# A reordered first stage, joined attention runs and fourteen instead of twelve gate pairs in a hybrid mixer layer

## The chip, the cores and the metric

The kernel runs on one core of one Trainium2 chip. The metric is the device time of one execution in microseconds (us). All data are float32; TensorE multiplies in float32r, and every operand is split into a high and a low part, so that one product of the mathematics is three matmuls (high x high, high x low, low x high).

## The reference

One layer of a diffusion backbone on 640 tokens: 512 sample tokens and 128 prompt tokens. In short:

```
mod = silu(c) @ w_ada + b_ada                    # sh1 sc1 g1 sh2 sc2 g2
h   = rmsnorm(x) * (1 + sc1) + sh1               # 640 x 1024
proj = h @ w_in                                  # ax ab ac | q ff fb i g | cq ck cv | du dv
y_a = ab * dwconv3(ac * ax)                      # gated convolution
y_b = hgrn2(q, ff, fb, i, g)                     # recurrence in both directions
y_c = attention(cq, ck, cv)                      # neighbourhood attention and context
y_d = du * (mixing of dv over 128 tokens)        # gated MLP
merged = sum over a, b, c, d of sigmoid(h @ w_gate + b_gate) * (y @ w_br)
x = x + g1 * (merged @ w_o)
h = rmsnorm(x) * (1 + sc2) + sh2
x = x + g2 * ((silu(g) * a) @ w_down),  (a, g) = dwconv3(h @ w_up)
```

Returned are the normalised x of both groups, the keys and values of the prompt, and the final states of the recurrence.

## The kernel before

**Layout.** h is kept transposed, features on the partitions, as `xh` (high part, 8 blocks of 128 features x 640 tokens) and `xl` (low part). A tile of a projection is 128 output features x 640 tokens, worked in two halves of 320 tokens (HC): 8 feature blocks x 3 matmuls x 2 halves = 48 matmuls of 320 columns. Weights come by DMA into one of three raw buffers (tag "raw"); `feat` (line 318) loads one and splits it: a ScalarE copy makes the high part, a VectorE subtraction (L329) the low part, in one of three weight buffers (tag "w"). `ahead` (line 1801) issues loads up to four units and preparations up to two units before use.

**The first stage.** x is loaded and normalised, transposed on TensorE, the first 16 column blocks of the modulation are computed from w_ada, and h is made. Meanwhile the first three tiles of w_in run on those feature blocks that are ready. The order of all this on every engine is a table written out by hand, BOOT (line 28), read token by token (line 1992) and kept as written. Its tokens: sq/sc (statistics and scaling of an x tile), tu/xo (transpose and copy out), ad, ev, tr, rd, md (one block of the modulation: product, copy, transpose, reduce, finish), adj, evj, ... (two blocks at once), hh/hm/hl (high part of h, h itself, low part), wh/wl (weight split), mikXY (one feature block k of tile i, high or low parts), warm (small matmuls that compute nothing). The order of the loads is LORD (line 22): numbers are blocks of w_ada (512 KB each), wih is half h of weight i (256 KB each). Behind them on SP's queue stand the small loads p2, lmask and four of st_in (lines 217 to 226), then the last four blocks of w_ada (L1981, regions A and B, used by adj3 and adj7).

**The middle.** The remaining sections of w_in follow in the order SECTIONS; jobs that are not plain products (HGRN, gMLP, convolution, attention, later columns of the modulation in `ada_cols`) are Python generators, which a clock of assumed TensorE time (`tick`, line 97) resumes between the products. The number that a job yields is the assumed time until it is resumed. The framework's scheduler then orders the instructions of each engine, except where the program asks to keep its order. Attention (line 701) works on 16 units (head x query block) in pairs; a round computes scores for the next pair (`s1`: TensorE L813 and L816, GpSimd L805, VectorE L820 and L822, ScalarE L823), normalises and transposes two units (`s2`: L829 to L835), and multiplies with the values (`s3`: L850, L856, L857).

**The gates.** There are 32 gate tiles, 8 for each branch in the order d, a, b, c. A plain gate tile (`gate_tile`, line 943) takes 48 matmuls for h @ w_gate and 12 for the branch. The 24 tiles of a, b and c run as 12 pairs (`g_pair`, line 1129): tiles n and n+4 share a scheme of seven instead of eight block products, on four quarters of h (two feature halves x two token halves) and sums of them. Each of the seven is 12 matmuls (L1098), and the branches take 24 (L1111). The operands x5, x6, x7 and x3 are sums of quarters, made in `g_operands` (line 992) from a copy of h in DRAM (`hdr`, line 931, stored at the end of the first stage, L2008), and split into high and low parts (`g_split`, L1023 and L1024). `g_operands` begins when the last d tiles have begun and the attention has ended. `gp_load` (line 1029) loads a pair's weights, `g_a`, `g_sums`, `g_b` and `g_c` prepare them, and from pair 0 on all engines keep the written order.

**After the gates** come w_o, the second normalisation, the up projection (in the same seven-product scheme, L1439) and the down projection (L1754). There, `low_dma` (line 1333) makes some low parts in another way: ScalarE writes minus the high part, and a DMA from GpSimd's queue adds the raw weight to it.

## Time and profile before

| | |
|---|---|
| median of 3 runs | 1042.53 us (1041.19 to 1042.62) |
| the profiled execution: time | 1042.9 us |
| its span, first to last instruction | 1041.1 us |
| mean granted TensorE clock | 0.996 |
| busy: TensorE, VectorE, ScalarE, GpSimd | 1021.4, 788.3, 528.9, 95.2 us |
| first stage ends (first L364 product) | 52.87 us |
| plain d tiles, last eight before the pairs | 280 to 357.7 us |
| attention ends (last L857) | 301.7 us |
| pairs | 357.7 to about 548 us |

The span holds the instructions; the execution's own time has some 1.8 us around them. The profile page gives busy times over the whole span; a view of waits says what an engine waited for; the chain follows back from the last instruction what released what; timelines list instructions in order of time, equal neighbours merged, with the start, the time that they take together, and in brackets the idle time before them. A name such as "L364 PE MATMUL g<-XH,w" is line 364, a matmul into PSUM tile g from XH and w. Line 146 is a helper that keeps the program's order: all first-stage instructions and all from the pairs on carry it, unless they have a line of their own.

### The profile page before, as it was taken

How to read it: one execution, taken by the hardware profiler on the slowest of the kernel's cores; microseconds unless marked ns; L12 is line 12 of the kernel's file. 1: busy time of each engine (PE TensorE's matmuls, PEld its weight loads, DVE VectorE, ACT ScalarE, POOL GpSimd, SP SyncE). 2: the span in 40 equal slices, each digit the busy share in tenths (PEclk: the TensorE clock that was granted, in tenths of full speed). 3: DMA queues.
4: the chain of work that ended last, by engine and by line, in shares of the span. 5: the costliest groups of instructions: out<-in, count | busy, mean ns of one | idle time of the engine just before them, and what ended most of it. 6: DMA issues, size and time to landing. Idle time of an engine off the chain costs nothing.

```text
span 1041.1 us, 18790 instructions
## 1 busy us (share of the span) xinstructions
PE 1021.4 (98%) x7638; PEld 962.9 (92%) x7638; DVE 788.3 (76%) x1280; ACT 528.9 (51%) x912; POOL 95.2 (9%) x139
## 2 busy tenths in 40 slices
PE   8899999999999999999999999999999999999997
PEld 6799989999889999999998899999999999888886
DVE  5559889789957467677768688998888887795834
ACT  6662343333243445445445377877677776632532
POOL 1000010201100000000000021211111111000201
PEclk9999999999999999999999999999999999999999
DMA  9954333453234122321258385666665558974212
GB/s 349 325 188 141 125 104 123 129 180 129 74 127 152 52 101 76 128 102 62 81 212 327 149 258 136 175 165 162 161 162 151 148 152 250 370 266 149 82 41 102
DMA packets 54296, 165.68 MB, mean 159 GB/s; under 512 B 7969, under 2 KB 14913, under 8 KB 52161
## 3 DMA queue, kind: packets, MB, share of 16 engines
q1 hardware_dynamic: 44432, 137.19, 37.8%
q0 software_dynamic: 9776, 27.28, 11.2%
q8 instruction: 60, 0.98, 0.4%
q14 instruction: 28, 0.22, 0.1%
HBM read 131.52 MB, written 21.52 MB: 147 GB/s over the span
## 4 chain that ended last, share of the span: by engine, by line
PE 91%; DVE 3%; DMA 3%; issue 1%; ACT 0%; SPq 0%; POOL 0%; POOLq 0%; DVEq 0%; ACTq 0%
PE g L364 19%; PE g L1439 19%; PE m L1098 14%; PE g L1754 8%; PE m L1754 6%; PE m L1439 5%; PE g L1111 4%; PE m L1234 3%; PE g L910 2%; PE g L1234 2%; PE m L525 1%; DMA S<-in_w_ada_dram 1%; PE m L850 1%; DMA B<-in_w_ada_dram 1%; DMA C<-in_w_ada_dram 1%; PE g L146 1%
## 5 line engine op out<-in xcount | busy, mean ns | idle before, releaser
L364 PE MATMUL g<-XH,w 128*128 128x320 f32 x832 | 201.2, 318 | 0.2 <-DVE MG L425 0.2
L364 PEld LDWEIGHTS g<-XH,w 128*128 128x128 f32 x832 | 142.9, 189 | 4.5 <-issue 3.7
L364 PE MATMUL g<-XL,w 128*128 128x320 f32 x416 | 129.7, 312 | 0.0
L364 PEld LDWEIGHTS g<-XL,w 128*128 128x128 f32 x416 | 78.9, 190 | 0.8 <-issue 0.5
L316 DVE TENSOR_TENSOR w<-raw,w 128x1024 fp32r<-128x1024 f32 x34 | 41.5, 1220 | 16.2 <-ACT w L315 15.5
L1754 PE MATMUL g<-w,XH 128*128 128x512 f32 (+1 forms) x216 | 47.5, 373 | 0.0
L315 ACT ACTIVATE w<-raw 128x1024 fp32r<-128x1024 f32 x34 | 35.8, 1052 | 20.5 <-PE g L1234 9.9
L1754 PEld LDWEIGHTS g<-w,XH 128*128 128x128 f32 x216 | 38.5, 188 | 7.6 <-ACT XH L1717 0.3
L1098 PE MATMUL m<-XH,w 128*128 128x320 f32 x192 | 45.0, 309 | 0.0
L146 DVE SCALAR_TENSOR_TENSOR X<-MG,p2t,X 128x641 f32<-128x641 f32 x44 | 38.9, 884 | 5.7 <-ACT X L146 4.8
L328 ACT ACTIVATE w<-raw 128x1024 fp32r<-128x1024 f32 (+1 forms) x26 | 29.4, 1130 | 22.2 <-PE g L364 7.5
L146 DVE SCALAR_TENSOR_TENSOR X<-X,p2t,X 128x641 f32<-128x641 f32 x44 | 38.9, 883 | 2.3 <-ACT X L146 1.0
L1754 PE MATMUL m<-w,XH 128*128 128x512 f32 (+1 forms) x180 | 40.2, 369 | 0.0
L1754 PE MATMUL g<-w,XL 128*128 128x512 f32 (+1 forms) x180 | 40.0, 373 | 0.0
L1439 PE MATMUL g<-XL,C 128*128 128x320 f32 x240 | 38.7, 310 | 0.4 <-ACT MG L146 0.4
L1439 PE MATMUL g<-XL,w 128*128 128x320 f32 x240 | 38.7, 310 | 0.2 <-DVE X L146 0.2
L1754 PEld LDWEIGHTS g<-w,XL 128*128 128x128 f32 x180 | 32.2, 188 | 6.8 <-DVE dt L1765 0.6
L329 DVE TENSOR_TENSOR w<-raw,w 128x1024 fp32r<-128x1024 f32 (+1 forms) x26 | 33.8, 1301 | 5.8 <-ACT w L328 5.6
L1439 PEld LDWEIGHTS g<-XL,C 128*128 128x128 f32 x240 | 35.9, 188 | 1.1 <-ACT MG L146 1.1
L1439 PEld LDWEIGHTS g<-XL,w 128*128 128x128 f32 x240 | 35.9, 188 | 0.8 <-issue 0.4
L1754 PEld LDWEIGHTS m<-w,XH 128*128 128x128 f32 x180 | 31.3, 189 | 5.3
L1754 PE MATMUL m<-w,XL 128*128 128x512 f32 (+1 forms) x150 | 33.2, 369 | 0.0
(544 smaller groups left out, 2704.9 us busy)
## 6 DMA issues: line engine op xcount, KB each, us to landing
raw<-in_w_up_dram SPq DMA_DIRECT2D x31, 512.0 KB, 5.1
raw<-in_w_gp_dram SPq DMA_DIRECT2D x18, 640.0 KB, 3.8
raw<-in_w_down_dram SPq DMA_DIRECT2D x22, 512.0 KB, 4.6
raw<-in_w_in_dram SPq DMA_DIRECT2D x19, 512.0 KB, 3.7
H<-in_w_adt_dram SPq DMA_DIRECT2D x16, 512.0 KB, 4.2
actd<-X POOLq DMA_DIRECT2D x22, 320.5 KB, 5.3
G<-in_w_up_dram SPq DMA_DIRECT2D x11, 512.0 KB, 4.8
X<-in_w_adt_dram SPq DMA_DIRECT2D x10, 512.0 KB, 4.1
```

The costliest lines, as they stand in the source:

```text
L146: r = f(*args, **kw)
L315: act(w[0], raw, AF.Copy)
L316: vec.tensor_tensor(w[1], raw, w[0].bitcast(F32), ALU.subtract)
L328: high = lambda: act(w[:, 0], raw, AF.Copy)
L329: low = lambda: vec.tensor_tensor(w[:, 1], raw, w[:, 0].bitcast(F32), ALU.subtract)
L364: mm(o, w[:, h, k0 + k, :], r(k)[:, s], start=(k == 0 and i == 0), stop=(k == kt - 1 and i == 2))
L910: mm(o, x(kx)[:, ts], w[:, h, k, :], start=(kx == 0 and i == 0), stop=(kx == 7 and i == 2))
L1098: mm(o, w[:, k, :], x[:, k, :], start=(first and k == 0 and j == 0), stop=(k == 3 and j == 2), skip_group_check=True)
L1111: mm(pb[:, c, 0:HC], w[:, h + k, :], y[:, x, k, s], start=(k == 0 and j == 0), stop=(k == 1 and j == 2))
L1234: mm(m, mh[k // 2][:, hx, k % 2, t * P:(t + 1) * P], wo[q][:, hw, k % 2, :], start=(k == 0 and i == 0), stop=(k == 7 and i == 2))
L1439: mm(o, w[:, k, :], x[:, k, :], start=(first and k == 0 and j == 0), stop=(k == 3 and j == 2), skip_group_check=True)
L1754: mm(acc[nh][t + c0 // 256][:, 0:c1 - c0], sl[k][hx][:, t * P:(t + 1) * P], w[:, hw, k, c0:c1], start=(kk_ == 0 and k == 0 and i == 0), st ...
```

## The change

- **First stage.** A new BOOT table of the same tokens. The first scalings of x come ahead of lbs and bada; 24 + 8 instead of 8 + 18 warm-up matmuls; the products are in another order (27 instead of 26 of the 72 pairs of products, and trj2, ahead of adj6). The loads of p2, lmask and st_in move from behind LORD to behind the stores of h at the end of the stage. h is stored by feature halves and token halves, four stores for two.
- **Fourteen pairs.** The d tiles 2, 3, 6 and 7 become two pairs in front of the others; the d tiles 0, 1, 4 and 5 stay plain. A d pair writes its product into the sum directly.
- **Operands of the pairs.** `g_operands` starts when the section cv is done. It loads three quarters of h into regions D and G as soon as attention has read cv, makes three sums after y_a (kept in written order), splits x7 once all scores are computed and x5, x6 after attention, then loads the fourth quarter over x5's source. Its sum for x3 is made in pair 0. y_b is kept in DRAM and brought back after the d pairs, y_c is stored by the attention.
- **Attention.** `s3` of a pair of units now stands directly ahead of `s1` of the next but one; a round yields 0.6 less.
- **Low parts.** The weights of ac, ax, ab and of the plain d tiles get their low part by `low_dma`.
- **Modulation columns 40 to 47**: gap 3 instead of 5, and 4 instead of 10 before the last step.

```diff
-sq0 sq1 lbs bada sc0a scv sc0b tu0a tu0b sq2 xo0a sc1b sc1a tu1b sq3 xo0b tu1a warm8 sc2a xo1a. sc2b tu2a xo1b
-sq4 tu2b sc3b ad0 sc3a xo2b. xo2a tu3b ev0. tu3a sc4b xo3b. ad8 sc4a xo3a. tr0 ev8 tu4a rd0 wh0a tr8 md0
...
+sq0 sq1 sc0a sc0b tu0a scv tu0b xo0a. sc1a sq2 bada tu1a warm24 xo0b xo1a sq3 sc1b lbs tu1b sc2a sq4
+sc2b tu2a xo1b tu2b ad0 xo2a. sc3a sc3b xo2b. tu3a sc4a ad8 ev0 wh0a sc4b tu4a xo3a tr0 ev8. xo4a. tr8
+rd0 tu4b rd8 md0 wh2a tu3b warm8 md8 xo4b hh0 ad1 wl2a xo3b. ev1 m20HH hm0 m00HH wh1a tr1 ad9 rd1 wl0a
+m20LH ev9. m10HH wl1a ad2 tr9 ev2. md1 m00LH rd9 m10LH hl0 ad10 md9 tr2 m00HL ev10 hh1 m10HL rd2 tr10
+md2 ad3 rd10 md10 m20HL hh2 hm1 m01LH m21LH m21HH hl1 m11LH ev3. m12HH wh0b m12LH hm2 m21HL wh1b m01HL
+wl0b m11HL wh2b m02HH m22HH wl1b m22LH m11HH hl2 ad11 tr3 ev11. wl2b m02LH m02HL m22HL rd3 tr11 md3 adj2
+rd11 md11 hh3 m12HL evj2 m01HH trj2 adj6 exp hm3 rdj2 hl3 m23HH m03HH m13LH evj6 m13HL m03HL mdj2 trj6
+lb m03LH adj3 rdj6 sig mdj6 m23HL evj3 m13HH trj3 m23LH hh4 rdj3 adj7 mdj3 hh5 m24LH evj7 m04LH trj7
...
+NPL = 2
+LOWD = ("ac", "ax", "ab", "d")
...
-    for r in (xreg0, xreg1):
-        vec.memset(r[:, 0:2 * XW].rearrange("p (i c) -> p i c", i=2)[:, :, D], (D * EPS) ** 0.5)
-    vec.memset(xe[4][:, D:XW], (D * EPS) ** 0.5)
+    for x in xe:
+        vec.memset(x[:, D:XW], (D * EPS) ** 0.5)
...
-    def feat(src, kt=8):
+    def feat(src, kt=8, dma=False):
...
-            low()
+            if dma:
+                low_dma(w[:, 1].rearrange("p a b -> p (a b)"), raw.rearrange("p a b -> p (a b)"))
+            else:
+                low()
...
-        R["yb"] = split_y("E", sg)
+        nc.sync.dma_start(ybd, split_y("D", sg).bitcast(F32))
         R["hgrn_done"] = True
-        R["yd"] = split_y("D", R["yt"])
+        R["yd"] = split_y("E", R["yt"])
...
         for u in range(0, 16, 2):
+            if u > 0:
+                s3(u - 2)
             if u < 14:
                 s1(u + 2)
-                yield HD[6]
+            else:
+                R["scores"] = True
+            yield HD[6]
             for i in range(2):
                 s2(u + i)
                 yield 1.2
-            s3(u)
-            yield HD[8]
+            yield HD[8] - 0.6
+        s3(14)
+        nc.sync.dma_start(ycd, yc.bitcast(F32))
...
-    PAIRS = [(bi, n) for bi in range(1, 4) for n in range(4)]
+    PAIRS = [(0, n) for n in range(NPL, 4)] + [(bi, n) for bi in range(1, 4) for n in range(4)]
...
     def g_operands():
-        while "yc" not in R:
+        while "cg" not in R:
             yield 1
...
+        d, g = region("D", [P, 2, 4, HC]), region("G", [P, 4, HC])
+        for x, h, c in ((d[:, 0], 0, 1), (d[:, 1], 1, 1), (g, 0, 0)):
+            nc.sync.dma_start(x, hdr[h, c])
+        while "ya" not in R:
+            yield 1
+        a21, a22, a11 = d[:, 0], d[:, 1], g
+        for o, x, y in ((a22, a21, a22), (a21, a11, a21), (a11, a22, a11)):
+            tc.keep_in_program_order(vec.tensor_tensor(o, x, y, ALU.subtract))
+            yield 2
...
+        for i, x, t, key in ((7, a21, "F", "scores"), (5, a22, "X1", "yc"), (6, a11, "X0", "yc")):
+            while key not in R:
+                yield 1
+            y = region(t, [P, 2, 4, HC], F32R)
+            gx["x"][i] = y[:, 0], y[:, 1]
             g_split(i, x)
             yield 1.5
+        nc.sync.dma_start(a22, hdr[1, 0])
+        gx["t3"] = a22, a11
...
-        r.append(region("G", [P, 10, P]) if p_ % 2 == 0 else rp.tile([P, 10, P], F32, tag="raw", name=nm("raw")))
+        r.append(region("G", [P, 10, P]) if p_ % 2 else rp.tile([P, 10, P], F32, tag="raw", name=nm("raw")))
...
-        return region("CBD"[i], [P, 5, 4, P], F32R)
+        return region("BCD"[i], [P, 5, 4, P], F32R)
...
-        ovec.tensor_tensor(c2(gt), pb, c2(gt), ALU.mult)
         mg = merged[n // 4][:, n % 4, :]
+        ovec.tensor_tensor(c2(gt if bi else mg), pb, c2(gt), ALU.mult)
+        if not bi:
+            return
         ovec.tensor_tensor(mg, mg, gt, ALU.add)
...
-            if PAIRS[q] == (1, 3):
-                R["yc"] = region("A", [P, 2, 2, T], F32R)
-                pool.dma_start(R["yc"], ycd)
+            if PAIRS[q] in ((0, 3), (1, 3)):
+                n_, t, y = ("yb", "E", ybd) if PAIRS[q][0] == 0 else ("yc", "A", ycd)
+                R[n_] = region(t, [P, 2, 2, T], F32R)
+                pool.dma_start(R[n_], y)
...
+        if q < 0:
+            t3, x6 = gx["t3"]
+            ovec.tensor_tensor(t3, t3, x6, ALU.add)
...
     for h in range(2):
-        nc.sync.dma_start(hdr[h], xT[h])
+        for c in range(2):
+            nc.sync.dma_start(hdr[h, c], xT[h][:, :, c * HC:(c + 1) * HC])
+    p2 = const.tile([P, 176], F32, name="p2t")
+    nc.sync.dma_start(p2, a["p2"])
...
```

More of the change, by code (lines that the diff above doesn't have):

```diff
@@ L216, in tile_step @@
             nc.sync.dma_start(adat[f // 2][:, f % 2], a["w_ada"][f])
-    p2 = const.tile([P, 176], F32, name="p2t")
-    nc.sync.dma_start(p2, a["p2"])
-    lmask = const.tile([P, 5, 32], U8, name="lmask")
-    lmr = region("G", [P, 5, 32])
-    nc.sync.dma_start(lmr, a["lmask"])
-    st_in = const.tile([P, 2, 2, 64], F32, name="st_in")
-    for par in range(2):
-        for d in range(2):
-            nc.sync.dma_start(st_in[64 * par:64 * par + 64, d],
-                              a["state_hgrn"][0, 0, d, par::2].rearrange("h k v -> k h v"))
     scv = const.tile([P, 8, 32], F32, name="scv")
@@ L245, in tile_step, with ada_cols @@
     growd = dram.tile([2, 16, P], F32, name="growd")
-    def ada_cols(fs, tag, homes, gap):
+    def ada_cols(fs, tag, homes, gap, last):
         cr = region(tag, [P, 2, D])
@@ L442, in evac_in @@
             act(dst[:, TS:T], ps[:, 1, 192:320], AF.Copy, scale=sc)
+    ybd, ycd = [dram.tile([P, 2, 2, T], F32, name=n) for n in ("ybd", "ycd")]
     def hgrn():
@@ L2007, in tile_step @@
     for h in range(2):
-        nc.sync.dma_start(hdr[h], xT[h])
+        for c in range(2):
+            nc.sync.dma_start(hdr[h, c], xT[h][:, :, c * HC:(c + 1) * HC])
+    p2 = const.tile([P, 176], F32, name="p2t")
+    nc.sync.dma_start(p2, a["p2"])
+    lmask = const.tile([P, 5, 32], U8, name="lmask")
+    lmr = region("G", [P, 5, 32])
+    nc.sync.dma_start(lmr, a["lmask"])
+    st_in = const.tile([P, 2, 2, 64], F32, name="st_in")
+    for par in range(2):
+        for d in range(2):
+            nc.sync.dma_start(st_in[64 * par:64 * par + 64, d],
+                              a["state_hgrn"][0, 0, d, par::2].rearrange("h k v -> k h v"))
     pool.tensor_copy(lmask, lmr)
```

53 lines of the change are left out of this document (15 added, 38 removed).

## The prediction

> **What bounds the kernel now.** First the page's busy times (us, share of the span, instructions):
>
> ```profile
> PE 1021.4 (98%) x7638; PEld 962.9 (92%) x7638; DVE 788.3 (76%) x1280; ACT 528.9 (51%) x912; POOL 95.2 (9%) x139
> ```
>
> TensorE is busy nearly all the time. Time can be gained in two ways only: fewer matmuls, or less waiting by TensorE. Next, the view of waits, TensorE alone (us in total, times, longest):
>
> ```profile
> PE m L146 <- DMA A<-in_w_ada_dram: 2.7, 3, 2.1
> PE m L146 <- DVE X L146: 2.4, 2, 1.6
> ...
> PE m L525 <- issue: 1.5, 1, 1.5
> PE m L146 <- DMA S<-in_w_ada_dram: 1.0, 1, 1.0
> ```
>
> Line 146 with A, S and X of w_ada and x is the first stage: 2.7 + 2.4 + 1.0 = 6.1 us of waits, most of it for w_ada, with 2.1 at one place. What it pays for one product is in the chain in order of time (start, length, what):
>
> ```profile
> 301.37 56.36 PE g L364 x383
> 357.74 8.80 PE m L1098 x60
> ...
> 407.01 7.04 PE m L1098 x48
> 415.81 5.28 PE m L1098 x36
> 422.86 7.04 PE m L1098 x48
> ```
>
> The 383 plain gate products take 56.36 us, 147 ns each, and the 48 of a pair 7.04 us, also 147 ns. From 407.01 to 422.86 one whole pair goes by in 15.85 us: 48 + 36 = 84 products of the seven-product scheme, and 24 of the branch in the gap (108 x 0.1467 = 15.84). So neither plain tiles nor pairs wait for anything, and a product is worth 0.147 us wherever it is removed.
>
> **The change, part by part.** *Two more pairs.* A plain gate tile is 48 + 12 = 60 products; two of them 120; a pair 108. Four tiles (35.2 us) become two pairs (31.7 us): **-3.5 us**. Bounds: -3.5 if the pairs start on time, and the waits below if not. The two new pairs write the sum directly, with one VectorE instruction fewer per tile.
>
> *The first stage.* Its transfers, first in the chain and then in the issue times of SP's queue:
>
> ```profile
> 14.07 8.42 DMA C<-in_w_ada_dram
> ...
> 22.51 10.15 DMA S<-in_w_ada_dram
> ...
> 32.68 5.29 DMA A<-in_w_ada_dram
> ...
> 38.10 1.07 PE m L146 x16
> ```
>
> ```profile
> 21.23 1.61 SPq L216 DMA_DIRECT2D S<-in_w_ada_dram  x2
> 23.79 0.33 SPq L218 DMA_DIRECT2D p2t<-in_p_dram  x1
> ...
> 26.28 3.83 SPq L225 DMA_DIRECT2D st_in<-in_state_hgrn_dram  x4
> 31.00 2.01 SPq L1981 DMA_DIRECT2D A<-in_w_ada_dram  x2
> ```
>
> Each transfer is issued just as an older one lands (C's at 14.07 + 8.42 = 22.49, the last S's at 22.51): a place in a fixed number of outstanding ones is waited for. p2, lmask and the four of st_in use six places, so A's second half goes out only at 32.68, when S has landed, and lands at 37.97. By the order of LORD, 6.5 blocks of 512 KB land in the 8.43 us before 22.49 (1.30 us each), and 6.5 in the 10.17 us up to S. Without the six, S lands 0 to 1.7 us earlier (10.17 - 6.5 x 1.30); I take 0.6, since the weight halves in between lag as well and the six carry few bytes. A's second half follows two blocks later, at 32.1 + 2.6 = 34.7 instead of 37.97. In the new table TensorE reaches adj3 at about 35.0 (adj6 from 32.1, 1.07 us as adj3 in the last row; six pairs of products at 0.29), so the wait of 2.1 us at that place goes. What is late next is adj6, still waiting for S. One more pair of products and the transposes trj2 stand ahead of it: 0.42 us less behind it. Sum: 0.6 + 2.1 + 0.4 = **-3.1 us**. The other edits of the table (first scalings ahead of lbs and bada, six more warm-up matmuls at 0.05 us) lie before S and are hidden by that wait. Bounds: 0, if the bytes and not the places set A's landing, to -6.1, all the waits.
>
> The six transfers now stand behind the stores of h, four halves of 640 KB instead of two of 1280 KB. SP's later loads (w_tok, cc, w_adt) queue behind six short issues, 6.3 us above (23.79 to 26.28 + 3.83). TensorE has units 3 to 5 in hand, 3 x 7 us of products, before it needs the next weight; lmask and st_in are read only by the HGRN job, tens of us later. Nothing. The memsets (five for three) are over before x lands.
>
> *Attention runs.* s3 of one pair of units now directly precedes s1 of the next. One iteration of the trace where the planner had kept them apart (upper rows), and one where it had joined them (lower rows), TensorE's timeline:
>
> ```profile
> 247.50 0.31 PE L364 MATMUL g<-XL,w 128*128 128x320 f32 x1
> 247.74 0.43 PE L850 MATMUL m<-B,X 128*64 128x128 f32 x2
> 248.10 0.56 PE L364 MATMUL g<-XH,w 128*128 128x320 f32 x2
> 248.51 0.31 PE L364 MATMUL g<-XL,w 128*128 128x320 f32 x1
> ...
> 249.09 0.31 PE L364 MATMUL g<-XH,w 128*128 128x320 f32 x1
> 249.32 0.70 PE L813 MATMUL m<-F 64*128 64x256 f32 x4
> 250.18 0.41 PE L364 MATMUL g<-XH,w 128*128 128x320 f32 x1
> 250.43 0.30 PE L364 MATMUL g<-XL,w 128*128 128x320 f32 x1
> ...
> 251.01 0.46 PE L364 MATMUL g<-XH,w 128*128 128x320 f32 x2
> ...
> 252.20 0.41 PE L364 MATMUL g<-XL,w 128*128 128x320 f32 x1
> 252.45 0.46 PE L364 MATMUL g<-XH,w 128*128 128x320 f32 x2
> ```
>
> ```profile
> 273.13 0.46 PE L364 MATMUL g<-XH,w 128*128 128x320 f32 x2
> ...
> 276.15 0.41 PE L364 MATMUL g<-XL,w 128*128 128x320 f32 x1
> 276.40 0.45 PE L364 MATMUL g<-XH,w 128*128 128x320 f32 x2
> ```
>
> Subtracting 0.147 per L364 product from the stretch around each run: apart, 247.50 to 248.51 costs 0.57, 249.09 to 250.43 1.05, 251.01 to 252.45 1.00, in sum 2.6 us; joined, 273.13 to 276.40 costs 2.83. So joining as the trace has it gains nothing. Of the 1.05, s1 itself has 250.18 - 249.32 = 0.86, which leaves 0.19 for entering and leaving a run. A joined run in clean order (all of s3, then all of s1) would be 2.62 less two such rims, 2.2. In the timeline four of the six iterations look like the lower rows, so the mean is 2.76. Bounds over six: +0.4 (all at 2.83) to -3.3 (all at 2.2). I take the upper rows' 2.6: **-0.9 us**. By the Trainium skill, "TensorEngine Tiling (Array Packing)", section "Key Properties", changing the tiling mode drains the array, so fewer runs should be cheaper. By that rule, the rim of 0.19 agrees with the trace, and the joined 2.83 does not.
>
> *Low parts by transfer.* Ten weights (ac, ax, ab, four of d) leave VectorE for a second ScalarE copy and an accumulating transfer from POOL's queue. Prices:
>
> ```profile
> L328 ACT ACTIVATE w<-raw 128x1024 fp32r<-128x1024 f32 (+1 forms) x26 | 29.4, 1130 | 22.2 <-PE g L364 7.5
> ...
> L329 DVE TENSOR_TENSOR w<-raw,w 128x1024 fp32r<-128x1024 f32 (+1 forms) x26 | 33.8, 1301 | 5.8 <-ACT w L328 5.6
> ```
>
> ```profile
> L805 POOL TENSOR_TENSOR B<-X 128x256 f32<-128x256 f32 x16 | 12.8, 819 | 72.4 <-DVE X L820 72.4
> ...
> w<-G POOLq DMA_DIRECT2D x11, 256.0 KB, 3.8
> ```
>
> VectorE gives up 10 x 1.3 = 13 us, ScalarE takes 10 x 1.13 = 11 us more. The last row is the same kind of transfer in the up projection: 3.8 us for half the size, so I count up to 7.6. A weight is ready 1.1 + 1.1 + 7.6 = 9.8 us after its preparation begins; the cover is two tiles (2 x 48 x 0.147 = 14.1 us) between that and its use, so TensorE sees nothing. Its raw buffer comes free later, when the transfer has landed rather than after VectorE's 1.3 us; the next load has the same two tiles. If the cover is gone, see the third rival.
>
> *Operands of the pairs.* The rows (VectorE, end of attention and the operand splits):
>
> ```profile
> 301.72 0.29 DVE L857 TENSOR_TENSOR C<-m,C 128x128 fp32r<-128x128 f32 x1 [1.69 <-ACT C L856]
> ...
> 312.85 1.49 DVE L1008 TENSOR_TENSOR B<-B 128x1280 f32<-128x1280 f32 x1 [5.08 <-DMA B<-hdr]
> ...
> 324.78 1.48 DVE L1024 TENSOR_TENSOR F<-B,F 128x1280 fp32r<-128x1280 f32 x1
> ```
>
> Now the operands are ready at 324.78 + 1.48 = 326.3, and pair 0 starts at 357.7: 31.4 us to spare, of which 35.2 us of plain tiles are taken. But the loads (11.1 us from 301.72 to 312.85) and three sums of 1.49 move ahead of the end of attention. Behind it stay the splits of x5 and x6 (two at 1.48, and as much on ScalarE), one 640 KB load (11.1 us at most, as above) and one sum: at most 6 + 11.1 + 1.5 = 18.6 us. Pair 0 comes 357.7 - 35.2 - 301.7 = 20.8 us after attention, and reads the last of these only at its seventh product, over 10 us into it: nothing. The stores of yb, yc and the reloads run beside products. Columns 40 to 47 of the modulation, made during the down projection, come at shorter gaps: the same VectorE work, a little earlier, beside products: nothing.
>
> **Sum.** -3.5 - 3.1 - 0.9 = -7.5. The profiled execution took 1042.9 us (span 1041.1): 1035.4. The median shown is 0.4 lower: **1035 us**.
>
> One term has either sign. After the wait of 1.5 us on L525 (issue) the clock falls:
>
> ```profile
> 142.00:146.00 4.00, 4.00 (x18) 4.00 (x18) 3.91 (x7) 2.94 (x4) 0.36 (x1) 0.57 0.20 76
> ```
>
> At a granted clock of 0.57 18 products run where 27 would: 1.4 us. Whether a run has it can go either way, +-1.4 on the range. The Trainium skill, "TensorE: Matmul & The Clock Gate", section "Part 1: The HAM clock gate", has the clock halved after a quiet window of some 3.4 us whose phase is free; the row agrees in length and depth, and no run shows the phase.
>
> **Rivals.** (1) *Clean joined runs*: each mode change avoided pays; 2.2 per iteration, -3.3 in place of -0.9: 1032.6. For it: the rim of 0.19. Against it: the joined row of 2.83. The tiling page named above would expect this. (2) *The first stage isn't changed in what matters*: bytes, not places, hold A's landing, or another load takes the places; only 0.4 to 1 us is gained: 1037.5. For it: the stretch before S was already slower than 1.30 per block with few small bytes. Against it: A's issue at 32.68 right as S lands. (3) *Slower, through POOL's queue*: an accumulating transfer queued behind an attention add (L805) waits for VectorE; eight rounds share 72.4 us of such waits, 9 each. The cover leaves 14.1 - 9.8 = 4.3 us for such a wait, or 8.1 with a landing in 3.8. From there on each us is one of TensorE's per weight; with 12 us of wait at five weights prepared during attention it loses 5 x (12 - 8.1) = 19.5 us: 1054.5. The gain is eaten from 9.6 us on. Against it: an add is issued a round ahead, when its buffer is mostly free again. (4) *A late start of the pairs*: G for pair 1 is reloaded only after the sum that reads it, and ScalarE's copy of it stands in order ahead of the copy on which product 7 waits: 11.1 us of loading against 7.0 us until that product: 4 us, 1039.
>
> **Chances.** Forecast (1033.5 to 1037) 0.48, rival 1 0.20, rival 2 0.13, rival 4 0.12, rival 3 0.05, nothing changes 0.02. 0.2% is about what a measurement of this kernel tells from no change. Faster by over 0.2% (below 1040.4) 0.91, within 0.03, slower 0.06. The range leaves out rival 3 and the outer parts of 1 and 4: 1031.5 to 1039.5.
>
> **What would show it.** Right: no TensorE wait for A in the first stage and its last product near 49.6 instead of 52.9; 14 periods of 15.85 us with pair 0 starting near 318; attention products in fewer runs. Wrong: a TensorE wait on L1098 at the first pair, on L364 for a DMA into w, or A still landing near 38.

## The result, and the profile after

The changed kernel takes 1040.74 us (median of 20 runs, 1038.75 to 1042.84), the kernel before on the same chips 1041.83 us (20 runs). One of the 20, at 2003 us, was disturbed; it lies outside these bounds and does not enter the ratio. The ratio is 0.9983, 95% interval 0.9973 to 0.9993: 1.8 us gained by the ratio (the medians are 1.1 us apart), where 7.5 were forecast; the time lies above the range given (1031.5 to 1039.5). The profiled execution took 1040.62 us (span 1038.8, before 1041.1).

Read off the timelines of both kernels, the span divides so (us; the end points are the first plain product, the first product of pair 0, the first of w_o and the end):

| stretch | before | after | difference | forecast |
|---|---|---|---|---|
| first stage | 52.87 | 49.67 | -3.20 | -3.1 |
| from there to pair 0 | 304.70 | 272.96 | -31.74 | -36.1 (four tiles of 8.8, and 0.9) |
| pairs | 190.19 | 223.13 | +32.94 | +31.7 (two pairs of 15.85) |
| w_o to the end | 493.34 | 493.01 | -0.33 | 0 |
| sum | 1041.10 | 1038.77 | -2.33 | -7.5 |

The first and the last row are as forecast. 4.4 us are missing before pair 0, and 1.2 in the pairs. TensorE is 98% busy as before, so the busy shares tell nothing; its view of waits does (us in total, times, longest):

```profile
PE m L830 <- DVE ast L826: 6.4, 1, 6.4
...
PE m L148 <- DMA B<-in_w_ada_dram: 1.2, 1, 1.2
...
PE m L1098 <- ACT gb L148: 1.0, 1, 1.0
```

One wait of 6.4 us is new, at the transposes of the attention's second step (L830, before the change L833), and one of 1.0 in a pair. The old ones of the first stage have fallen, for A from 2.7 to 0.6, for X from 2.4 to 1.0, and S's 1.0 is gone; B's 1.2 has come instead.

**The wait of 6.4 us.** TensorE waits for VectorE, so VectorE's timeline comes next (start, length, what, in brackets the idle time before it and what ended it):

```profile
227.59 0.28 DVE L231 TENSOR_SCALAR modt<-ar,bada,cst 128x2 f32<-128x2 f32 x1
228.05 0.16 DVE L826 RECIPROCAL ast<-ast 128x1 f32<-128x1 f32 x1 [0.18 <-ACT X L820]
228.25 0.42 DVE L827 TENSOR_SCALAR X<-X,ast 128x384 f32<-128x384 f32 x1
234.43 1.23 DVE L259 SCALAR_TENSOR_TENSOR junk<-A,S 128x1024 bf16<-128x1024 f32 x1 [5.76 <-DMA A<-in_w_adt_dram]
...
235.59 0.16 DVE L826 RECIPROCAL ast<-ast 128x1 f32<-128x1 f32 x1
```

VectorE stands idle for 5.76 us in front of L259, the product of a w_adt tile that makes a column of the modulation. Nothing of the attention needs it, but it stands ahead in VectorE's order, and the reciprocal of L826, for which TensorE waits, stands behind it. The load of that tile is what is late. From the tile view of A between 195 and 240, the kernel before and the changed one:

```profile
DMA to landing us min/median/max: 3.4/3.4/3.5
```

```profile
DMA to landing us min/median/max: 3.4/3.4/11.3
```

The same 512 KB take 3.5 us at most before and 11.3 here. VectorE comes to the product at 228.67, 5.6 us after the load's issue at 223.12: that is the slack of this load, and whatever it takes beyond it VectorE waits. What is issued ahead of it, SP's queue and then GpSimd's, in the changed kernel:

```profile
212.28 0.33 SPq L637 DMA_DIRECT2D ybd<-D  x1
215.35 0.33 SPq L999 DMA_DIRECT2D G<-hdr  x1
...
219.06 2.91 SPq L999 DMA_DIRECT2D D<-hdr  x2
222.69 0.33 SPq L311 DMA_DIRECT2D raw<-in_w_in_dram  x1
223.12 0.53 SPq L248 DMA_DIRECT2D A<-in_w_adt_dram  x1
```

```profile
213.63 0.86 POOL L148 DMA_DIRECT2D w<-raw  x1 [8.17 <-ACT w L148]
222.61 0.86 POOL L148 DMA_DIRECT2D w<-raw  x1 [8.12 <-ACT w L148]
```

The store of y_b, the three early loads of h and the accumulating transfers of the low parts (w<-raw) are all new here. The windows view (of each row, the last three figures are the granted TensorE clock, the DMA engines' busy share and GB/s), before and after:

```profile
208.00:234.00 26.00, 26.00 (x192) 24.24 (x191) 21.27 (x45) 9.77 (x23) 1.43 (x2) 1.00 0.56 182
```

```profile
208.00:234.00 26.00, 25.54 (x189) 24.03 (x187) 14.82 (x31) 13.09 (x26) 3.17 (x4) 1.00 0.99 294
240.00:244.00 4.00, 4.00 (x16) 3.85 (x16) 3.55 (x7) 0.00 (x0) 0.70 (x1) 0.50 0.98 241
```

The DMA engines go from 0.56 to 0.99 busy. The view of the DMA queues for the same window (packets, MB, share of 16 engines) says by what, in the changed kernel:

```profile
q1 hardware_dynamic: 2339, 6.14, 67.8%
q0 software_dynamic: 409, 1.47, 31.3%
```

The first is SyncE's queue, which has 55.7% in the kernel before; the second holds the accumulating transfers, and before it moves nothing in this window. So of the 43 points added the transfers are 31, and SyncE's queue, with the loads of h and the store of y_b, is 12.

And the wait has a tail: in the row from 240 to 244 the clock is 0.50, and 16 products run where 27 of 0.147 us would. The half clock begins at 237.34, inside the wait, and ends at 244.17, 4.3 us after it; at half speed that costs about another 2 us. The Trainium skill, "TensorE: Matmul & The Clock Gate", section "Part 1: The HAM clock gate", has the clock halved after an idle window of 3.4 us, until a busy window of that length has passed; here it falls 3.8 us into the wait and stays low for 6.8 us, which agrees.

**The pairs.** From the chain in order of time:

```profile
325.51 1.41 DVE D L148
...
326.94 5.49 DMA G<-in_w_gp_dram
332.46 0.69 DVE S L148
...
334.12 1.22 ACT C L148 x2
335.34 0.26 issue
335.61 0.43 ACT gb L148
336.07 3.93 PE m L1098 x25
```

```profile
341.77 7.04 PE m L1098 x48
...
531.85 7.04 PE m L1098 x48
```

From 341.77 to 531.85 twelve periods take 15.84 us each: the pairs themselves are as forecast. The first alone is longer, by the wait of 1.0: G can only be loaded after the sum that reads it (D, until 326.92), and ScalarE's copies for pair 1 (C<-S, made from G) stand ahead of the copy gb, for which TensorE's next product waits. That is the fourth rival, at 1 us instead of 4.

**Attention.** A joined run of the changed kernel, TensorE's timeline:

```profile
251.28 0.31 PE L357 MATMUL g<-XH,w 128*128 128x320 f32 x1
251.53 0.66 PE L847 MATMUL m<-B,X 128*64 128x128 f32 x8
252.01 0.39 PE L847 MATMUL m<-B 128*64 128x128 f32 x4
252.33 0.70 PE L810 MATMUL m<-F 64*128 64x256 f32 x4
252.87 0.39 PE L813 MATMUL m<-B,F 64*128 64x128 f32 x4
...
253.44 0.31 PE L357 MATMUL g<-XL,w 128*128 128x320 f32 x1
```

All twelve value products, then all eight of the scores: 253.44 - 251.28 less two L357 products of 0.147 is 1.86 us, against 2.6 to 2.83 before. Four of the six runs are like this (1.86 to 2.02), two are still mixed (2.5 and 2.3). Counted in the same way, the six cost about 12.4 us together, before 16.5. So the attention gains some 4 us and not 0.9: the first rival's mechanism, and more than its 3.3. The last value products, half of them clean now, give another 0.7 (2.55 for 3.30). The account closes to within the reading of these rows: -3.2 for the first stage, -4.2 and -0.7 for the attention, +6.4 and about +2 for the wait and its tail, -3.5 for two pairs, +1.1 in the first pair: -2.1, where -2.33 is measured.

### The profile page after: what moved, and what is told of

It is laid out like the page before. It is cut to its first block, busy times and chain, and to the rows that moved or that the text cites. A ratio compares the mean times of both kernels' runs of the same rounds, so it can differ in the third digit from the quotient of the medians.

```text
span 1038.8 us, 18832 instructions
## 1 busy us (share of the span) xinstructions
PE 1015.9 (98%) x7620; PEld 958.6 (92%) x7620; DVE 790.1 (76%) x1299; ACT 537.2 (52%) x931; POOL 106.4 (10%) x150
## 3 DMA queue, kind: packets, MB, share of 16 engines
q0 software_dynamic: 11360, 34.36, 14.7%
## 4 chain that ended last, share of the span: by engine, by line
PE 91%; DMA 3%; DVE 3%; ACT 1%; issue 1%; SPq 0%; POOL 0%; POOLq 0%; DVEq 0%; ACTq 0%
PE g L1446 20%; PE m L1098 16%; PE g L357 15%; PE g L1761 8%; PE m L1761 6%; PE m L1446 5%; PE g L1111 5%; PE m L1241 3%; PE g L915 2%; PE g L1241 2%; PE m L148 2%; PE g L148 1%; DMA A<-in_w_adt_dram 1%; PE m L521 1%; DMA A<-in_w_ada_dram 1%
## 5 line engine op out<-in xcount | busy, mean ns | idle before, releaser
L357 PE MATMUL g<-XH,w 128*128 128x320 f32 x704 | 174.6, 322 | 0.0
L357 PEld LDWEIGHTS g<-XH,w 128*128 128x128 f32 x704 | 123.0, 192 | 2.5 <-issue 1.2
L357 PE MATMUL g<-XL,w 128*128 128x320 f32 x352 | 110.1, 313 | 0.0
L357 PEld LDWEIGHTS g<-XL,w 128*128 128x128 f32 x352 | 67.5, 192 | 0.0
L1098 PE MATMUL m<-XH,w 128*128 128x320 f32 x224 | 52.6, 309 | 1.0 <-ACT gb L148 1.0
L148 ACT ACTIVATE w<-raw 128x1024 fp32r<-128x1024 f32 (+3 forms) x46 | 38.2, 850 | 3.3 <-DMA raw<-in_w_in_dram 2.3
L1098 PEld LDWEIGHTS m<-XH,w 128*128 128x128 f32 x224 | 38.3, 188 | 1.2 <-ACT gb L148 1.2
L1446 PE MATMUL g<-XL,w 128*128 128x320 f32 x240 | 38.7, 310 | 0.0
L1446 PEld LDWEIGHTS g<-XL,w 128*128 128x128 f32 x240 | 35.9, 188 | 0.5 <-ACT MG L148 0.3
L1098 PE MATMUL m<-XL,w 128*128 128x320 f32 x112 | 34.6, 309 | 0.0
```

Source lines behind the costliest of these rows:

```text
L148: r = f(*args, **kw)
L357: mm(o, w[:, h, k0 + k, :], r(k)[:, s], start=(k == 0 and i == 0), stop=(k == kt - 1 and i == 2))
L1098: mm(o, w[:, k, :], x[:, k, :], start=(first and k == 0 and j == 0), stop=(k == 3 and j == 2), skip_group_check=True)
L1446: mm(o, w[:, k, :], x[:, k, :], start=(first and k == 0 and j == 0), stop=(k == 3 and j == 2), skip_group_check=True)
```

## The experiments

Theory T at the start: the early loads of h fill the DMA engines, the w_adt tile is late, and VectorE's order hands that to TensorE. Rivals: Ra, the accumulating transfers fill them; Rb, VectorE's order makes the wait whatever lands when. Ratios are against the kernel before in the same series (it had 1042.7 to 1043.0 us there); 0.001 is 1.04 us.

| run | median us | ratio, 95% interval | TensorE's longest wait in the attention |
|---|---|---|---|
| changed kernel | 1040.74 | 0.9983 (0.9973 to 0.9993) | 6.4 |
| e1_loads_late | 1037.56 | 0.9943 (0.9926 to 0.9960) | 4.0 |
| e1b_loads_last | 1037.02 | 0.9943 (0.9927 to 0.9958) | 3.6 |
| e12_loads_held | 1039.39 | 0.9962 (0.9947 to 0.9977) | 3.0, at the end |
| e2_low_vec | 1036.14 | 0.9933 (0.9910 to 0.9957) | 0.5 |
| e9_loads_twice | 1043.88 | 1.0007 (0.9990 to 1.0025) | 11.0 |
| e8_low_only (from before) | 1040.54 | 0.9978 (0.9966 to 0.9991) | under 0.3 |
| e3_sum_early | 1039.42 | 0.9968 (0.9954 to 0.9982) | 6.4 |
| e4_stage_only (from before) | 1038.82 | 0.9962 (0.9944 to 0.9979) | under 0.3 |
| e4b_table_only (from before) | 1041.09 | 0.9979 (0.9968 to 0.9990) | under 0.3 |
| e4c_moved_only (from before) | 1040.28 | 0.9971 (0.9959 to 0.9983) | under 0.3 |
| e6_joined_only (from before) | 1041.58 | 0.9983 (0.9970 to 0.9996) | under 0.3 |
| e14_joined_kept (from before) | 1039.51 | 0.9973 (0.9962 to 0.9985) | 0.2 |
| e10_vec_sum | 1035.19 | 0.9916 (0.9902 to 0.9930) | under 0.3 |
| e16_vec_sum_kept | 1034.02 | 0.9917 (0.9901 to 0.9932) | 0.2 |
| e17_held_sum_kept | 1037.46 | 0.9949 (0.9931 to 0.9966) | 2.8, at the end |
| e18_twelve_kept | 1038.54 | 0.9954 (0.9942 to 0.9966) | 0.5 |

**Loads later.** Two tries that only told the planner to wait:

```diff
+            if u == 6:
+                R["mid"] = True
-        while "cg" not in R:
+        while "mid" not in R:
...
+            yield 4
```

> The changed kernel with one edit: the three quarter loads of h for the pairs' sums start about eight attention steps later. Theory T (the early loads fill the DMA engines, so the load of w_ada's column tile lands 10.8 us after its issue instead of 3.2, VectorE stands in its order at the column product from 228.67 to 234.43, and TensorE waits 6.4 us behind it): the load lands in 3 to 6 us, TensorE's wait on VectorE at the second attention step is under 1.5 us, the stretch from 240 to 244 no longer runs at a granted clock of 0.50, and the time falls by 5 to 8 us, to about 1034, unless the later loads make the first pair's operands late. Rival Ra (the accumulating transfers of the low parts fill the engines): the load still takes about 10 us and the wait stays above 5 us; no change in time, 1040 to 1041.5. Rival Rb (VectorE's planned order alone makes the wait, with whatever load): the wait stays near 6 us although the load lands early. In this kernel the column product still stands ahead of the two reciprocals on VectorE, so a wait that goes, goes because of the load.

e1b has `while "scores" not in R` in that place, without the `yield 4`.

> The changed kernel with the three quarter loads of h, and so their sums, held until all scores are computed, some 60 us later than in the changed kernel; the accumulating transfers stay. The earlier try moved them by only 4 us. Theory C (transfers and early loads together): the DMA share from 208 to 234 falls from 0.99 to about 0.75, w_ada's column tile lands in 4 to 7 us, TensorE's wait on VectorE there is under 1.5 us; the median falls to 1035 to 1037, unless the first pair now waits for its operands. Theory Ra (transfers alone): the wait stays above 4 us and the median above 1039.

Neither did what it said. SP's timeline of e1b:

```profile
215.37 0.33 SPq L999 DMA_DIRECT2D G<-hdr  x1
...
224.04 0.54 SPq L999 DMA_DIRECT2D D<-hdr  x1
224.67 1.27 SPq L248 DMA_DIRECT2D A<-in_w_adt_dram  x1
226.00 0.69 SPq L999 DMA_DIRECT2D D<-hdr  x1
```

G still goes out where it did (215.37 here); the two D loads move by 4 to 5 us only, and the last one now comes after A. With that A lands 9.3 us (e1) and 7.8 us (e1b) after its issue instead of 11.3, the wait is 4.0 and 3.6, and the time falls by about 4 us against the changed kernel, by the ratios. So the D loads matter, whether by their bytes or by their place ahead of A; the test of the theory fell short, since they were still on the way beside it.

**No accumulating transfers:**

```diff
-LOWD = ("ac", "ax", "ab", "d")
+LOWD = ()
```

> The changed kernel with the low parts of the pairs' sums made on VectorE by itself, without accumulating transfers on GpSimd's queue. Theory T: the loads of h and the store of the half sum are still there, so the load of w_ada's column tile still takes 7 to 11 us and TensorE's wait at the second attention step stays at 4 to 7 us; the time is 1039 to 1043 (VectorE has more to do). Rival Ra (the accumulating transfers are what fills the DMA engines): the load lands in about 4 us, the wait falls under 2 us, and the time is 1033 to 1036. Rival Rb (order): the wait moves with the order that VectorE has here, and not with the load's time.

The edit takes the transfers from the weights of ac, ax, ab and the plain d tiles; the pairs' sums, of which the expectation speaks, had none. Waits, VectorE's timeline and window of e2:

```profile
PE m L830 <- DVE ast L826: 0.5, 1, 0.5
```

```profile
230.61 1.23 DVE L259 SCALAR_TENSOR_TENSOR junk<-A,S 128x1024 bf16<-128x1024 f32 x1 [1.25 <-DMA A<-in_w_adt_dram]
```

```profile
208.00:234.00 26.00, 26.00 (x191) 24.50 (x190) 21.01 (x41) 11.94 (x27) 2.87 (x4) 1.00 0.70 246
```

The early loads are all there, the wait is not: theory T as stated falls. The DMA share is 0.70, though A still takes 7.8 us, as long as in e1b, where TensorE waits 3.6. The difference is the slack: in e2 VectorE comes to the product 6.6 us after the load's issue, in e1b 3.2 us. So of the 4.5 us that VectorE waits less than in the changed kernel (1.25 for 5.76), 3.5 are the faster landing and 1.0 is that it comes later itself. What the transfers cost the DMA engines stands in the pages' rows of the software queue (packets, MB, share of 16 engines), changed kernel and e2:

```profile
q1 hardware_dynamic: 44864, 138.50, 39.1%
q0 software_dynamic: 11360, 34.36, 14.7%
```

```profile
q0 software_dynamic: 9920, 28.59, 11.6%
```

Ten transfers: 14.7% of 1038.8 less 11.6% of 1035.0 is 32.6 us of all 16 engines, 3.3 us each, for 5.77 MB, which is 177 GB/s; the other queue moves 138.5 MB in 406 us, 341 GB/s. A byte of these transfers costs the engines about twice a byte of SyncE's queue. Whether the addition costs it, or the way from SBUF to SBUF, no run parts.

**Transfers alone**, in the kernel before:

```diff
-                plain(lambda s=s, n=n: feat(a["w_in"][OFF[s] // P + n]),
+                plain(lambda s=s, n=n: feat(a["w_in"][OFF[s] // P + n], dma=s in LOWD),
...
-                return feat(a["w_gate"][GI[br] * 8 + n], 10)
+                return feat(a["w_gate"][GI[br] * 8 + n], 10, br in LOWD)
```

> The kernel before with one part of the change alone: the low parts of the weights ac, ax, ab and of all eight d tiles by a ScalarE copy and an accumulating transfer. It has fourteen transfers where the changed kernel has ten, and no early loads of h. Theory Ra (the accumulating transfers alone fill the DMA engines enough): w_ada's column tile and the next weights land 7 us or more after their issue, TensorE waits 3 to 7 us on VectorE in the attention's second step, and the time is 3 to 7 us above the kernel before, 1045 to 1049. Theory C (only transfers and early loads together saturate; in the changed kernel the DMA share was 0.99 from 208 to 234, before 0.56, without the transfers 0.70): no new TensorE wait over 1.5 us, the time within 1.5 us of the kernel before. The prediction's own step said: nothing.

```profile
208.00:234.00 26.00, 26.00 (x195) 24.53 (x194) 17.71 (x40) 12.72 (x26) 4.05 (x5) 1.00 0.94 236
```

The DMA share in this window is 0.94, and still A lands within 4.6 us, and TensorE waits for nothing. The slack is 7.1 us here, but 4.6 would have met the changed kernel's 5.6 as well. So Ra alone falls too. Theory C is left: transfers and early loads together. (It is even 2.3 us faster than before by the ratio: half of its groups of value products come out clean, see below, and counted as above its attention runs cost 2.8 us less in all.)

**The loads doubled:**

```diff
             nc.sync.dma_start(x, hdr[h, c])
+            nc.sync.dma_start(x, hdr[h, c])
```

> The changed kernel with each of the three quarter loads of h issued twice, one after the other on SyncE's queue: the suspected load doubled, with the result unchanged. Theory T (these loads and the store fill the DMA engines ahead of w_ada's column tile): the tile lands 3 to 6 us later than in the changed kernel, TensorE's wait at the second attention step grows from 6.4 to 9 to 12 us, and the time rises by 3 to 6 us, to 1044 to 1047. Rival Ra (accumulating transfers): the tile lands within 1 us of before, the wait stays at 6 to 7 us, the time rises by under 1.5 us. Rival Rb (order alone): the wait stays at 6 to 7 us.

The wait grows to 11.0 as expected; against the changed kernel the time is 2.5 us up by the ratios, less than the 3 to 6. A lands at 246.5, 12 us later than in the changed kernel and not 3 to 6: it is issued only at 234.87, behind the doubled loads on SP's queue, so this run shows both the traffic and the queue.

**The loads really held back**, by a write into their regions that needs a late result:

```diff
+            if u == 12:
+                R["hold"] = yc[:, 0, 1, 16:17].bitcast(F32)
...
+            act(x[:, 0, 0:1], R["hold"], AF.Copy)
             nc.sync.dma_start(x, hdr[h, c])
```

> The changed kernel with the three quarter loads of h really held back: ScalarE first writes one element per partition of a result of the attention's eleventh unit into the loads' regions, so that the loads can only start some 40 us later. The two earlier tries moved the loads by 4 to 5 us only. The accumulating transfers and the order of VectorE stay. Theory C (accumulating transfers and early loads together fill the DMA engines): w_ada's column tile lands 4 to 6 us after its issue, TensorE's wait on VectorE at the second attention step is under 1 us, nothing runs at half clock behind it, and the median falls to 1033 to 1035. Theory Ra (the transfers alone) or Rb (VectorE's order alone): the wait stays at 3.5 us or more and the median at 1037 or more. If the late loads make the first pair's operands late, a new wait stands at the first pair's products instead.

The old wait is gone: window, then waits, then VectorE's timeline, then a window of e12:

```profile
208.00:234.00 26.00, 26.00 (x194) 24.75 (x194) 20.36 (x44) 15.24 (x31) 4.61 (x6) 1.00 0.85 244
```

```profile
PE m L847 <- DVE B L832: 4.9, 2, 3.0
```

```profile
288.30 1.49 DVE L1007 TENSOR_TENSOR D<-D 128x1280 f32<-128x1280 f32 x1 [5.35 <-DMA D<-hdr]
...
292.58 0.69 DVE L148 TENSOR_TENSOR S<-raw,raw 128x512 f32<-128x512 f32 x1 [2.32 <-DMA raw<-in_w_gp_dram]
```

```profile
295.00:299.00 4.00, 4.00 (x16) 3.74 (x15) 4.00 (x4) 1.97 (x4) 0.00 (x0) 0.50 0.84 164
```

A lands 5.3 us after its issue and the second step waits for nothing: theory C holds at the disputed place, with the product still ahead of the reciprocals in VectorE's order, so Rb falls. But the median is 1039.4, not 1033 to 1035. Now the half sum stands in VectorE's order ahead of a copy of the attention, waits 5.35 us for its own load, TensorE loses 4.9 us, and 6.1 us behind it (to 299.89) run at a clock of 0.50. It is the same mechanism at another place: an instruction kept in order waits for a load, and the attention stands behind it.

**The first pair's sum early:**

```diff
         nc.sync.dma_start(a22, hdr[1, 0])
+        yield 6
+        vec.tensor_tensor(a22, a22, a11, ALU.add)
...
-        if q < 0:
-            t3, x6 = gx["t3"]
-            ovec.tensor_tensor(t3, t3, x6, ALU.add)
```

> The changed kernel with the one half sum that reads the buffer of w_in's next part moved from the pinned work of the first pair to just behind the fourth quarter load. Theory (the sum at 325.43 holds the reload of that buffer, the reload the copy on ScalarE, and that the seventh product's operand at 335.6): TensorE's wait on ScalarE at 334.8 to 336.1 in the first pair goes, the period of the first pair is 15.85 us, and the time falls by 1.0 to 1.3 us, to about 1039.5. Rival (the copy on ScalarE is late by its own place in the order, not by the load): the wait stays at about 1.1 us and the time stays within 0.3 us. The 6.4 us wait of the attention is not touched by either.

The wait at L1098 (L1100 here) is gone from the list, pair 0 to w_o takes 1.4 us less (221.76 for 223.13), and the ratio falls by 0.0015, with intervals that overlap. The trace shows the fourth rival's mechanism; the time alone would not.

**The first stage by parts.** e4 has the table and the moved loads in the kernel before, e4b and e4c one of them each.

> The kernel before with the first stage of the change alone: the new table and the six small loads moved behind the stores of h. The prediction's term: 3.1 us less; the changed kernel's trace has its last first-stage product 3.2 us earlier. If that reaches the end undiminished: 3.0 to 3.4 us below the kernel before, the last first-stage product at 49.5 to 49.8. Rival: later work waits for the moved loads or for something that does not come earlier with the stage, and under 2 us reach the end.

> The kernel before with the new table of the first stage alone; the six small loads stay where they were. The prediction's step: the small loads hold places among the outstanding transfers, so w_ada's last block lands late; the table mainly fills time. By that, A still lands near 37.9, the wait for A and its like stays at 2 to 4 us, the last first-stage product comes at 51.5 to 53, and the median falls by 0 to 1.3 us. Rival (the table does it): the last product at 50.5 or earlier, 2.4 us or more gained.

> The kernel before with the six small loads moved behind the stores of h, and the old table. By the prediction's step: A lands 1 to 3 us earlier, near 35 to 36.7, the wait for A falls under 1.5 us, and the last first-stage product comes at 50 to 51; the median falls by 2 to 3 us. Rival (places do not matter, only bytes): A lands as before and the median falls by under 0.7 us.

The first plain product comes at 49.83, 50.51 and 51.21, before at 52.87. The gain of 4.0 us by the ratio reaches the end. With the loads moved alone A's second half lands at 34.08 (34.7 forecast) and no wait for A is left, but the old table now waits for VectorE; the waits of e4c and of e4b:

```profile
PE m L146 <- DVE X L146: 2.7, 2, 2.3
```

```profile
PE m L146 <- DMA A<-in_w_ada_dram: 1.2, 3, 0.7
```

In these traces the table alone gains 2.4 us, the moved loads alone 1.7, both together 3.0; by the ratios it is 2.2, 3.0 and 4.0, each known to 1 to 2 us. With the table alone, and the six small loads where they were, A's second half already lands at 35.82, before at 37.97. So the places in the queue are real, but the table is worth about as much, and the two overlap.

**Attention runs.** e6 has the changed kernel's `for u` loop in the kernel before; e14 adds

```diff
+        pin = tc.keep_in_program_order
...
-                    mm(mo[64 * hh_:64 * hh_ + 64, 0:P], v, ptt[(u + hh_) % 3][:, j * P:(j + 1) * P],
-                       start=(j == 0), stop=(j == 2))
+                    pin(mm(mo[64 * hh_:64 * hh_ + 64, 0:P], v, ptt[(u + hh_) % 3][:, j * P:(j + 1) * P],
+                           start=(j == 0), stop=(j == 2)))
```

and the same around the two score products.

> The kernel before with the joined attention order alone. The prediction's term: 0.9 us less (2.6 us per iteration). Its first rival: clean joined runs, 3.3 us less (2.2 per iteration). The changed kernel's trace shows joined runs at 1.86 to 2.02 us against 2.6 to 2.83 before, about 0.8 us in each of six iterations: 4 to 5 us less, 1037.5 to 1038.5 where the kernel before takes 1042.5. If the gain was an effect of something else in the change: within 1.5 us of the kernel before.

> The kernel before with the joined attention order and, on top, TensorE's score and value products kept in written order, so that no score product stands inside a group of value products. With the joined order alone the planner still mixes them (a run costs 2.83 us, the median was 1.4 us below the kernel before). Theory M (what costs is the change between the two tile shapes inside a run; the joining itself gives only a rim of 0.19): every run costs 1.9 to 2.5 us, and the median falls by 2.5 to 4.5 us against the kernel before. Rival (the gain seen in the changed kernel's attention comes from VectorE being freed, not from the order of the products): runs cost less but the median stays within 0.7 us of the joined order alone.

A run of e6 (upper rows begin and lower end it):

```profile
247.50 0.31 PE L364 MATMUL g<-XH,w 128*128 128x320 f32 x1
247.74 0.43 PE L850 MATMUL m<-B,X 128*64 128x128 f32 x2
248.10 0.70 PE L813 MATMUL m<-F 64*128 64x256 f32 x2
248.72 0.54 PE L850 MATMUL m<-B,X 128*64 128x128 f32 x5
...
250.62 0.31 PE L364 MATMUL g<-XL,w 128*128 128x320 f32 x1
```

The source joins s3 and s1, but the planner puts two score products among the value products: 2.83 us. The six runs together cost about 0.9 us less than before, just as forecast; by the ratio the gain is 1.8 us, give or take 1.3. In e14 the score products no longer stand among the value products, but the planner puts plain products behind the first two value products, and such a run costs 0.56 + 1.84 = 2.40. The six are about 2.5 us cheaper than before, and the ratio gives 2.8 (2.5 to 4.5 expected); against e6 it falls by 0.0010, with intervals that overlap. The clean 1.86 appears in the kernels with accumulating transfers (the changed one, e1b, e12, e3), and the clean but unjoined form, 1.00 + 1.05, in part of e8; without transfers (before, e2, e6, e10) the runs are mixed. So the transfers both give and take: with them the planner's runs come out cleaner, and their traffic helps to make the wait. Why the planner's order depends on them, by the work they take from VectorE or otherwise, is not shown.

**Mended kernels**, all from the changed one: e10 is e2 with e3's edit, e16 that with e14's, e17 has the edits of e12, e3 and e14.

> The changed kernel without accumulating transfers and with the half sum of the first pair made early; the attention's products as the planner puts them (mixed runs of 2.83 us). It parts the two terms in the best kernel so far (ratio 0.9917 with kept order, 0.9933 without the sum and the kept order). If the early sum gives its 1.1 us here: ratio 0.9921 to 0.9925, and the kept order is worth 0.5 to 1 us. If the kept order gives more: ratio 0.9930 or above.

> The changed kernel without accumulating transfers for the plain tiles, with the half sum of the first pair made early, and with the attention's score and value products kept in written order. Theory M and the theory of the first pair's wait: against the same kernel with neither (1036.1 median, ratio 0.9933) the sum gives 1.1 us and the clean order 1.5 to 3 us: 1032 to 1033.5. If the planned order of VectorE costs instead: 1035 or more.

> The changed kernel with three mends at once: the loads of h held back, the half sum of the first pair made early, the attention's products kept in written order; the accumulating transfers stay. If the three waits found are all that the change lost: the wait of 6.4 us with its half clock (about 7.5), the wait of 1.1 at the first pair and about 1 us of mixed attention runs go, and the median is 1030.5 to 1033. If another wait takes their place, or VectorE or the DMA engines become the bound behind them: 1034 or more.

e10 and e16 come out alike, 0.9916 and 0.9917: about 8.7 us faster than before, and 6.9 faster than the changed kernel. Against e2 that is 1.8 us for the early sum (1.1 expected; the intervals overlap), and nothing measurable for the kept order, for which e16 was expected 1.5 to 3 us better. e17 keeps the transfers and holds the loads, and misses its 1030.5 to 1033: it has e12's wait of 4.9 us at the attention's end, and one of 2.1 at the old place. A lands in 7.0 us there though the loads are held (5.3 in e12), and the slack is 4.0 us (5.6 in e12), since the attention comes 1.8 us earlier. So a small wait is possible without the early loads; what else makes A slower in e17 is not shown.

**Twelve pairs** in e16:

```diff
-NPL = 2
+NPL = 4
...
         r[1] = gp_load(1)
+        R["yb"] = region("E", [P, 2, 2, T], F32R)
+        pool.dma_start(R["yb"], ybd)
```

> The best kernel so far (no accumulating transfers, early sum, kept order) with twelve pairs instead of fourteen: four of the d tiles run plain again, y_b comes back ahead of the pairs. The prediction's term: two pairs more are worth 3.5 us (24 products of 0.147). If they are worth that in full: 3.2 to 3.8 us above the same kernel with fourteen pairs, ratio 0.9948 to 0.9953. If plain tiles give room for work that the pairs have to wait for: under 2.5 us.

0.9954 against 0.9917: two pairs are worth 3.9 us, give or take 2, with 3.5 forecast.

## Why the prediction was wrong

- **First stage, -3.1:** right in its sum (-3.2), and in A's landing (34.7 forecast, 34.12 measured in the changed kernel), so rival 2 did not come. Its split was not: the table's other edits, put at nothing, gain 2.4 us alone and bring A's landing to 35.82 by themselves. That the sum fits so well is in part luck.
- **Two pairs, -3.5:** right; 3.9 by e18 (within its error), periods of 15.84.
- **Attention, -0.9:** the mechanism was the first rival's. The rim of 0.19 was read rightly: clean runs cost 1.00 + 1.05 apart and 1.86 joined. But the joined row of 2.83 was taken for joining as such, when it showed a mixed order. Joined alone gains what was forecast (0.9 by the runs of e6, 1.8 by its ratio), with clean order some 4.
- **Low parts by transfer, and the operands' early loads, each "nothing":** the step that failed. Each was priced by itself, the transfer by a row from the up projection (up to 7.6 us, against 6.4 to 9.8 for those issued from 201 to 223) and the loads as traffic "beside products". By itself each is next to nothing, as predicted: e8 has no wait with the transfers alone, e2 one of 0.5 with the loads alone. But both fall in the same 20 us, the transfers use the DMA engines twice as long per byte, and a third party pays: a w_adt tile that neither step named, 11.3 us under way, with an in-order VectorE instruction behind which the attention stood. That is 6.4 us, and about 2 more at half clock. The prediction asked whether the weights' own cover would hold, and it did; it did not ask who else loads then, nor what stands behind such a load on its engine. The Trainium skill, "DMA: Bandwidth & Descriptors", section "Issuing engines are not separate DMA queues", has all issuers share the same 16 engines; the window at 0.99, split 68 to 31 between the two queues, agrees.
- **Rival 3 (GpSimd's queue)** did not come: no weight was late behind an attention add. **Rival 4 (late start of the pairs)** did, at 1.0 us for 4: G landed 5.5 us after its issue, half of the 11.1 assumed.
- **Clock term, +-1.4:** the wait on L521 (issue) is in all traces, the half clock behind it in 13 of 18; in e16 the clock there was 1.00, which is part of its low time in the profiled run.

The chance for faster by over 0.2% was put too high for the same reason: the measured 0.17% lies at the edge of what can be told from no change.

## What to carry to other kernels

Add up the traffic of all moved and added transfers for the window in which they fall, and look there for the load with the least slack (the time from its issue until its first reader is ready), whoever owns it. Then read what stands behind its first reader on that in-order engine: an instruction that has no hurry itself can hold the one that has. And when a change joins parts in the source, check in the trace that the order on the engine is joined too.

## What the runs showed of the hardware

An accumulating transfer from GpSimd's queue occupies the DMA engines about twice as long per byte as the transfers of SyncE's (177 against 341 GB/s of engine time, changed kernel and e2). Value products of 64 columns, when all twelve stand together, start in pairs 6 to 7 ns apart, each pair 102 to 154 ns after the last (changed kernel, 251.5 to 252.2); with another tile shape in between, 200 to 320 ns go by at each change (before, 273.5 to 275.3). Behind each TensorE wait of 2.8 us or more in the attention, 3.4 to 6.2 us run at half clock (changed kernel, e1, e1b, e3, e9, e12, e17, at two places); the whole stretch at half clock lasts 3.4 us once, 13.7 us in e9, and 6.8 us in the other five.
